# Log-decay rows read back from DRAM instead of picked by matmuls, in a hybrid encoder layer

## The chip, the cores and the metric

The kernel runs on one core of a Trainium2 chip. The metric is the time of one execution on the device in microseconds; the median of several runs is compared. The engines are named as in the profile: PE (TensorE: matmuls; PEld its weight loads), DVE (VectorE), ACT (ScalarE), POOL (GpSimd) and SP (SyncE, which here only issues DMAs). Each engine works through its own instructions in order and waits on semaphores for the others.

## The reference, cut to what matters

One layer of an encoder on 528 tokens (16 learned ones and 512 of input) of width 2048: a normalization, one input projection, three branches (gated linear attention, differential attention, and a Mamba-2 state-space branch, SSD), one output projection and a last normalization. The change lies in the SSD branch: 16 heads in two groups of eight, two directions, chunks of 128 tokens, a depthwise convolution of five taps on 1536 channels.

```python
xbc = silu(depthwise_conv(xbc, conv_w, conv_b))          # 5 taps, 12 tiles of 128 channels
dt = softplus(dt_raw.reshape(B, L, 2, HEADS) + dt_bias)  # one dt per direction and head
a = dt * (-exp(A_log))
y = bidirectional(ssd_chunk_scan, (xs, dt[:, :, 0], a[:, :, 0], Bm, Cm),
                  (xs, dt[:, :, 1], a[:, :, 1], Bm, Cm), SSD_CHUNK)

def ssd_chunk_scan(x, dt, a, Bm, Cm):                    # per chunk of 128
    acs = cumsum(a, axis=2)
    seg = acs[:, :, :, None] - acs[:, :, None, :]
    decay_ts = exp(where(causal, seg, -inf))
    scores = einsum('bctgn,bcsgn->bctsg', Cm, Bm)[..., None] * decay_ts
    y_diag = einsum('bctsgr,bcsgrp->bctgrp', scores, x * dt[..., None])
    ...
```

## The kernel before, in words

The tokens' normalized features are kept transposed, as two float32r parts (`uh` and `ul`, 16 tiles each), so a projection takes three matmuls for each weight tile: high by high, high by low, low by high. Each weight tile is loaded by SP (`wraw`, two buffers), its high part is made on ACT (`whi`, line 72 within `wsplit`) and its low part on DVE (`wlo`, line 146); these two are traced at high priority. `t1` projects 128 columns over all tokens in two chunks of 48 matmuls; `t2` projects 512 columns for 512 tokens.

In the SSD branch the decays of both directions are combined into one tile for each head. `at` is the log decay per token and head. `Xs` holds sums of it with tokens over the partitions, `Xr` the same sums as rows: 32 rows (direction and head) of 512 tokens, as a float32r part and its remainder. In `ssd_decay(g)`, for each of the eight heads of a group:

- POOL makes `dtm`, the tile of dt factors, in two operations of 128 x 512 (lines 439 and 440);
- for each direction a matmul with a one-hot column of `pkr` (line 445) spreads the head's row of `Xr` over all 128 partitions in PSUM;
- for each chunk ACT adds `Xs` of the first direction (line 448), and DVE subtracts that of the second and takes the minimum (line 450);
- ACT takes the exponential (line 452) and DVE multiplies by `dtm` (line 453). The result `m` is kept for the group.

`ssd_group(g, em)` then runs the convolutions, multiplies `m` by the scores (line 552), and computes outputs and states. `conv_tile` copies a projected tile to `xp`, takes the first tap on DVE (line 411), four more taps on DVE (line 413), a tanh on ACT (line 415) and a product on DVE (line 416).

`dtm`, `sg` and most passing tiles of these stages share the tag "w", which has eight slots; `m` has the tag "ya" with twelve. No order is written out by hand: a planner takes the instructions in the program's order as priority, simulates them with its own costs, and fixes each engine's order, SP's queue too. Work that stands later in the program, such as the projections for `z` after the SSD branch, can be put where an engine would be free.

Of the kernel before, what the change touches and what calls it, by code (L numbers as in the profile page):

```python
# [8 lines left out]
F32 = mybir.dt.float32  # L9
F32R = mybir.dt.float32r  # L10
U32 = mybir.dt.uint32
AF = mybir.ActivationFunctionType
ALU = mybir.AluOpType
# [4 lines left out]
P = 128  # L18
NM = 16
S = 512  # L20
L = NM + S
# [6 lines left out]
NC = 4  # L28
# [6 lines left out]
M_ID, M_LE, M_GE, M_ONE, M_DU, M_GT, M_LT, M_LEC, M_GEC = range(9)  # L35


def mm(nc, out, lhsT, rhs, start=True, stop=True):
    nc.tensor.matmul(out, lhsT=lhsT, rhs=rhs, start=start, stop=stop)  # L39
# [2 lines left out]
@with_exitstack  # L42
def encoder_kernel(ctx, tc, x, meta, rel_bias, final_norm_w, norm_w, w_in, w_out, gla_wa2, gla_ba,
                   gla_norm_w, diff_lambda, diff_norm_w, conv_w, conv_b, A_log, dt_bias, ssd_D,
                   ssd_norm_w, masks, umask, onehot, pick, out):
    nc = tc.nc
    ctx.enter_context(nc.allow_low_precision(reason="operands split exactly into two float32r parts"))
    ctx.enter_context(nc.allow_non_contiguous_dma(reason="small parameter rows"))
# [1 line left out]
    const = ctx.enter_context(tc.tile_pool(name="const", bufs=1))  # L50
# [4 lines left out]
    dram = ctx.enter_context(tc.tile_pool(name="dram", bufs=1, space=DRAM))  # L55
# [3 lines left out]
    def pm():  # L59
        return ps_m.tile([P, 512], F32, name="pm", tag="pm")  # L60

    def pb():
        return ps_b.tile([P, 512], F32, name="pb", tag="pb")
# [4 lines left out]
    def slot(tag, shape=None, dt=F32, name=None):  # L68
        return wk.tile(shape or [P, 532], dt, name=name or tag, tag=tag, bufs=BUFS[tag])

    def cpy(out, in_, **kw):
        nc.scalar.activation(out, in_, AF.Copy, **kw)  # L72

    tt = nc.vector.tensor_tensor
    ts_ = nc.vector.tensor_scalar
    stt = nc.vector.scalar_tensor_tensor
    gtt = nc.gpsimd.tensor_tensor
# [33 lines left out]
    mtile = const.tile([P, 5, P], F32, name="masks")  # L111
# [62 lines left out]
    def t1(cols, tokens=True):  # L174

        acc = (pm(), pm()) if tokens else (pm(),)
        for kc in range(2):
            ks = slice(kc * 8, kc * 8 + 8)
            c0 = cols[0][0]
            hi, lo = wsplit(lambda raw: [(raw, win[:, ks, c0:c0 + P])], [P, 8, P])  # L180
            for kk in range(8):
                k = kc * 8 + kk
                for n, (wt, ur) in enumerate(((hi, uh[k]), (hi, ul[k]), (lo, uh[k]))):
                    first = k == 0 and n == 0
                    last = k == KT - 1 and n == 2
                    if tokens:
                        mm(nc, acc[0][:, 0:HA], wt[:, kk, :], ur[:, 0:HA], first, last)
                        mm(nc, acc[1][:, 0:HB], wt[:, kk, :], ur[:, HA:L], first, last)
                    else:
                        mm(nc, acc[0], wt[:, kk, :], ur[:, NM:L], first, last)  # L190
        return acc if tokens else acc[0]

    def take(dst, acc, rows=slice(0, P), **kw):

        cpy(dst[rows, 0:HA], acc[0][rows, 0:HA], **kw)
        cpy(dst[rows, HA:L], acc[1][rows, 0:HB], **kw)
# [112 lines left out]
    nc.sync.dma_start(mtile[:, 1:5], masks[1:5].rearrange("m p q -> p m q"))  # L309
    mstr = slot("w", [P, 4, P], name="mstr")  # L310
    nc.sync.dma_start(mstr, masks[5:9].rearrange("m p q -> p m q"))
    pks = slot("w", [P, 32], name="pks")
    nc.sync.dma_start(pks, pick.rearrange("p z h -> p (z h)"))
    pkr = const.tile([P, 32], F32R, name="pkr")
    cpy(pkr, pks)
    cwx = const.tile([P, 5, 8], F32, name="cwx")
    cwb = const.tile([P, 5, 4], F32, name="cwb")
    cvv = vt[:, 16:76].rearrange("p (k j) -> p k j", j=12)
    cbb = const.tile([P, 12], F32, name="cbb")
# [30 lines left out]
    dtt = const.tile([P, 5, 32], F32, name="dtt")  # L350
# [24 lines left out]
    Xs = const.tile([P, 2, 4, 16], F32, name="Xs")  # L375
    px = pb()
# [1 line left out]
        mm(nc, px[:, z * 64:(z + 1) * 64], mstr[:, 2 + z], at[:, 0:4, z * 16:z * 16 + 16])  # L378
    ts_(Xs[:, 0].rearrange("p c h -> p (c h)"), px[:, 0:64], -1.0, None, ALU.mult)
    nc.vector.tensor_copy(Xs[:, 1].rearrange("p c h -> p (c h)"), px[:, 64:128])  # L380
    Xr = slot("w", [P, S], F32R, name="Xr")
    for z in range(2):
        px = pb()
        for c in range(NC):
            mm(nc, px[0:32, c * P:(c + 1) * P], at[:, c, :], mstr[:, 2 + z])
        zs = slice(32 * z, 32 * z + 32)
        cpy(Xr[zs], px[0:32])
        tt(Xr[64 + 32 * z:96 + 32 * z], px[0:32], Xr[zs].bitcast(F32), ALU.subtract)
    xem = const.tile([NM, 16], F32, name="xem")
    nc.scalar.activation(xem, pd[0:NM, 384:400], AF.Exp)  # L390
    tt(xem, xem, dtt[0:NM, 4, 0:16], ALU.mult)
# [3 lines left out]
    dtd = const.tile([P, 4, 16], F32, name="dtd")  # L395
# [5 lines left out]
    def conv_tile(j, tag, cps=None):  # L401

        if cps is None:
            cps = t1([(C_X + j * P, P, 0)])
        xp = slot("ev", name="xp")
        nc.gpsimd.memset(xp[:, 0:2], 0.0)
        nc.gpsimd.memset(xp[:, 530:532], 0.0)
        take(xp[:, 2:530], cps)
        cw = cwx[:, :, j] if j < 8 else cwb[:, :, j - 8]
        acc = slot(tag, [P, L], name="acc")  # L410
        ts_(acc, xp[:, 0:L], cw[:, 0:1], cbb[:, j:j + 1], ALU.mult, ALU.add)  # L411
        for k in range(1, 5):
            stt(acc, xp[:, k:k + L], cw[:, k:k + 1], acc, ALU.mult, ALU.add)  # L413
        th = slot("ev", [P, L], name="th")
        nc.scalar.activation(th, acc, AF.Tanh, scale=2.0 if j < 8 else 1.0)
        stt(acc, th, 1.0, acc, ALU.add, ALU.mult)
        return acc
# [8 lines left out]
    def bc(ap):  # L426
        return ap[:, :, None].broadcast_to([P, 4, P])
# [5 lines left out]
    def ssd_decay(g):  # L433

        em = []
        for h in range(g * 8, g * 8 + 8):

            dtm = slot("w", [P, 4, P], name="dtm")
            gtt(dtm, mtile[:, None, M_LE, :].broadcast_to([P, 4, P]), bc(dtd[:, :, h]), ALU.mult)
            gtt(dtm, dtm, bc(dtt[:, 0:4, 16 + h]), ALU.add)  # L440

            sg = slot("w", [P, 4, P], name="sg")
            for z in range(2):
                px = pb()
                mm(nc, px, pkr[:, z * 16 + h:z * 16 + h + 1].broadcast_to([P, P]), Xr)
                for c in range(NC):
                    if z == 0:
                        nc.scalar.activation(sg[:, c], px[:, c * P:(c + 1) * P], AF.Identity, bias=Xs[:, 0, c, h:h + 1])
                    else:
                        stt(sg[:, c], px[:, c * P:(c + 1) * P], Xs[:, 1, c, h:h + 1], sg[:, c], ALU.subtract, ALU.min)  # L450
            m = slot("ya", [P, 4, P], name="m")
            nc.scalar.activation(m, sg, AF.Exp)
            tt(m, m, dtm, ALU.mult)  # L453
            em.append(m)
        return em
# [113 lines left out]
    for g in range(2):  # L569
        ssd_group(g, ssd_decay(g))  # L570
# [177 lines left out]
    for g in range(2):  # L748
        snw = slot("st", [P, 512], name="snw")
        nc.gpsimd.dma_start(snw, ssd_norm_w[:, g * 512:(g + 1) * 512].broadcast_to([P, 512]))  # L750
        acc = t2(win, C_Z + g * 512, uh, ul, NM)
# [129 lines left out]
    for o_, i, col in ((og, 0, C_GG), (od, 1, C_DG)):  # L881
        for c in range(NC):
            gtt(v4(o_[c]), v4(o_[c]), gn[:, i][:, None, :].broadcast_to([P, 4, P]), ALU.mult)
        acc = t2(win, col, uh, ul, NM)
# [9 lines left out]
    for k in korder:  # L894
        pt = pb()
        for c in range(NC):
            src, j = (og[c], k) if k < 4 else ((od[c], k - 4) if k < 8 else (yacc[(k - 8) // 4, c], k % 4))
# [29 lines left out]
    for b in range(3):  # L927
        acc = t2(wout, b * 512, mh, ml, 0, korder)
# [6 lines left out]
    acc = [pm() for _ in range(NC)]  # L935
# [40 lines left out]
def _consts():  # L976

    import numpy as np
    i = np.arange(P)
    r, c = i[:, None], i[None, :]  # L980
    masks = np.stack([r == c, r <= c, r >= c, r + c >= 0, r + c >= 0, r > c, r < c,
                      (r <= c) * 1.0 - (r < 64), (r >= c) * 1.0 - (r >= 64)]).astype(np.float32)
    masks[M_DU] = 1.0 + np.eye(P, dtype=np.float32)
    umask = (r > c).astype(np.uint32)
    rel = np.arange(NTAB) - (S + NM - 1)
    n = np.abs(rel)
    nf = np.maximum(n, 1).astype(np.float32)
    large = 8 + (np.log(nf / np.float32(8)) / np.float32(math.log(16.0)) * np.float32(8)).astype(np.int32)
    large = np.minimum(large, 15)
    bucket = np.where(rel > 0, 16, 0) + np.where(n < 8, n, large)  # L990
    onehot = (np.arange(32)[:, None] == bucket[None, :]).astype(np.float32)
    onehot = np.concatenate([onehot, onehot, 0 * onehot])
    pick = np.zeros((P, 2, 16), np.float32)
    for z in range(2):
        for h in range(16):
            pick[48 * z + h, z, h] = pick[64 + 48 * z + h, z, h] = 1.0
    return {'masks': masks, 'umask': umask, 'onehot': onehot, 'pick': pick}


def build(arrays):  # L1000
    import concourse.bacc as bacc
    nc = bacc.Bacc("TRN2", target_bir_lowering=False, num_devices=1, dynamic_dma_scratch_size=8192)
    args = [nc.dram_tensor(k, v.shape, mybir.dt.from_np(v.dtype), kind="ExternalInput").ap()
            for k, v in arrays.items()]
    args.append(nc.dram_tensor("out_0_dram", (S, D), F32, kind="ExternalOutput").ap())
    with tile.TileContext(nc, schedule_with_timeline_sim=True) as tc:
        encoder_kernel(tc, *args)
    return nc
# [10 lines left out]
```

## Time and profile before

| What | Value |
|---|---|
| median of 3 runs | 920.37 us (917.81 to 920.91) |
| profiled execution | 917.57 us, its span 915.8 us |
| PE busy | 876.9 us, 96% |
| DVE busy | 554.0 us, 60% |
| ACT busy | 383.7 us, 42% |
| POOL busy | 183.7 us, 20% |
| moved by DMA | 88.33 MB, mean 96 GB/s |

The span runs from the first to the last instruction of the profiled execution. Busy times are sums over an engine's instructions; matmuls are pipelined, so one record of a matmul is longer than the step from one to the next. The shares are means over stages with different limits.

### The profile page before, as it was taken

What the parts mean: (1) busy time and instruction counts of PE and PEld (TensorE: products, weight loads), DVE (VectorE), ACT (ScalarE), POOL (GpSimd) and SP (SyncE); (2) the same over time, 40 slices, a digit from 0 to 9 for tenths busy, and PEclk for the clock granted to TensorE, in tenths of its full rate; (3) what the DMA queues carried; (4) which work ended last, traced back from release to release, by engine and by line L of the source; (5) the groups of instructions that cost most, each with busy time, mean ns of one, the idle gap of its engine ahead of it and who ended that gap; (6) DMA issues with size and microseconds to landing.
All of it is one profiled execution on the core that took longest, in us unless ns stands there. A gap on an engine that the chain in (4) does not pass through costs nothing.

```text
span 915.8 us, 14461 instructions
## 1 busy us (share of the span) xinstructions
PE 876.9 (96%) x5737; PEld 779.9 (85%) x5737; DVE 554.0 (60%) x1049; ACT 383.7 (42%) x753; POOL 183.7 (20%) x215
## 2 busy tenths in 40 slices
PE   3898999999999999999999999999999999999996
PEld 3898999997778888899999999988888888888884
DVE  6669977999957568853642467775552543232334
ACT  6555434335534376734232345553342333132322
POOL 2006203549246302010040000000120002020200
PEclk9999999999999999999999999999999999999998
DMA  9422332221223234123337333324223532322225
GB/s 238 106 70 69 76 87 71 64 76 46 70 72 91 79 85 115 47 70 93 87 77 203 84 82 84 85 81 136 81 81 103 173 123 90 109 92 92 93 92 184
DMA packets 99587, 88.33 MB, mean 96 GB/s; under 512 B 8223, under 2 KB 75415, under 8 KB 99519
## 3 DMA queue, kind: packets, MB, share of 16 engines
q1 hardware_dynamic: 95183, 77.06, 29.8%
q0 software_dynamic: 1456, 5.10, 1.9%
q10 hardware_dynamic: 2880, 5.24, 1.7%
q8 instruction: 45, 0.74, 0.3%
q14 instruction: 23, 0.19, 0.1%
HBM read 83.18 MB, written 6.34 MB: 98 GB/s over the span
## 4 chain that ended last, share of the span: by engine, by line
PE 75%; DVE 12%; ACT 4%; issue 4%; DMA 2%; SPq 1%; POOL 1%; ACTq 0%; POOLq 0%; DVEq 0%
PE pm L39 65%; PE pb L39 7%; DVE acc L413 2%; DVE wlo L146 2%; DMA xt<-in_x_dram 2%; PE pb L898 1%; PE pb L852 1%; DVE sg L450 1%; ACT whi L72 1%; DVE acc L411 1%; DVE xs L459 1%; DMA gn<-in_diff_norm_w_dram 1%; SPq L228 1%; DVE m L552 1%; DVE m L453 0%
## 5 line engine op out<-in xcount | busy, mean ns | idle before, releaser
L146 DVE TENSOR_TENSOR wlo<-wraw,whi 128x1024 fp32r<-128x1024 f32 (+1 forms) x128 | 163.7, 1280 | 212.6 <-ACT whi L72 212.3
L72 ACT ACTIVATE whi<-wraw 128x1024 fp32r<-128x1024 f32 (+1 forms) x134 | 137.2, 1025 | 297.6 <-PE pm L39 237.4
L39 PE MATMUL pm<-ul,whi 128*128 128x272 f32 (+2 forms) x960 | 224.4, 300 | 0.0
L39 PE MATMUL pm<-uh,whi 128*128 128x272 f32 (+2 forms) x960 | 221.9, 298 | 0.6 <-ACT uh L72 0.6
L39 PE MATMUL pm<-uh,wlo 128*128 128x256 f32 (+2 forms) x928 | 214.6, 297 | 1.2 <-DVE wlo L146 0.7
L39 PEld LDWEIGHTS pm<-uh,whi 128*128 128x128 f32 x960 | 154.8, 189 | 6.7 <-ACT uh L72 1.2
L39 PEld LDWEIGHTS pm<-ul,whi 128*128 128x128 f32 x960 | 155.0, 189 | 5.1 <-issue 0.2
L39 PEld LDWEIGHTS pm<-uh,wlo 128*128 128x128 f32 x928 | 149.7, 189 | 6.8 <-DVE wlo L146 2.1
L39 PE MATMUL pm<-wlo,uh 128*128 128x512 f32 x256 | 102.5, 401 | 2.3 <-DVE wlo L146 2.3
L39 PE MATMUL pm<-whi,ul 128*128 128x512 f32 x256 | 101.3, 397 | 0.0
L39 PE MATMUL pm<-wlo,mh 128*128 128x512 f32 x256 | 100.6, 394 | 0.0
L39 PE MATMUL pm<-whi,ml 128*128 128x512 f32 x256 | 100.5, 394 | 0.0
L39 PE MATMUL pm<-whi,uh 128*128 128x512 f32 x256 | 95.0, 398 | 0.0
L39 PE MATMUL pm<-whi,mh 128*128 128x512 f32 x256 | 90.3, 395 | 0.0
L129 POOL TENSOR_TENSOR rs_r<-rs_v,mhalf 128x1 f32<-128x1 f32 (+1 forms) x28 | 20.5, 734 | 273.2 <-DVE rs_v L128 191.9
L39 PEld LDWEIGHTS pm<-wlo,uh 128*128 128x128 f32 x256 | 48.6, 190 | 13.3 <-DVE wlo L146 2.8
L39 PEld LDWEIGHTS pm<-whi,ml 128*128 128x128 f32 x256 | 48.2, 188 | 11.4
L39 PEld LDWEIGHTS pm<-whi,ul 128*128 128x128 f32 x256 | 48.6, 190 | 10.5
L39 PEld LDWEIGHTS pm<-whi,mh 128*128 128x128 f32 x256 | 48.1, 188 | 11.1
L39 PEld LDWEIGHTS pm<-wlo,mh 128*128 128x128 f32 x256 | 48.1, 188 | 10.9
L39 PEld LDWEIGHTS pm<-whi,uh 128*128 128x128 f32 x256 | 48.2, 189 | 10.7
L932 POOL TENSOR_TENSOR hx<-hx,fw 128x512 f32<-128x512 f32 x12 | 18.1, 1537 | 164.6 <-ACT junk L919 164.6
(304 smaller groups left out, 1197.7 us busy)
## 6 DMA issues: line engine op xcount, KB each, us to landing
wraw<-in_w_in_dram SPq DMA_DIRECT2D x96, 512.0 KB, 3.9
wraw<-in_w_out_dram SPq DMA_DIRECT2D x30, 512.0 KB, 3.6
xt<-in_x_dram SPq DMA_DIRECT2D x16, 256.0 KB, 5.2
hx<-in_x_dram ACTq DMA_DIRECT2D x16, 256.0 KB, 3.9
out_dram<-hx SPq DMA_DIRECT2D x16, 256.0 KB, 2.8
tabr<-tabd POOLq DMA_DIRECT2D x4, 520.0 KB, 7.0
bt<-tabr POOLq DMA_DIRECT2D x4, 456.0 KB, 3.6
fw<-in_final_norm_w_dram ACTq DMA_DIRECT2D x4, 256.0 KB, 4.3
```

Of the source, the lines that this page charges most:

```text
L39: nc.tensor.matmul(out, lhsT=lhsT, rhs=rhs, start=start, stop=stop)
L72: nc.scalar.activation(out, in_, AF.Copy, **kw)
L129: gtt(r[0:rows, 0:cols], v[0:rows, 0:cols], mhalf[0:rows, 0:cols], ALU.pow)
L146: tt(lo, raw, hi.bitcast(F32), ALU.subtract)
L228: nc.sync.dma_start(raw[:, :, 32 * i:32 * i + 32], win[:, k0:k0 + 8, c0:c0 + 32])
L411: ts_(acc, xp[:, 0:L], cw[:, 0:1], cbb[:, j:j + 1], ALU.mult, ALU.add)
L413: stt(acc, xp[:, k:k + L], cw[:, k:k + 1], acc, ALU.mult, ALU.add)
L450: stt(sg[:, c], px[:, c * P:(c + 1) * P], Xs[:, 1, c, h:h + 1], sg[:, c], ALU.subtract, ALU.min)
L459: tt(lo, src, hi.bitcast(F32), ALU.subtract)
L552: tt(m, m, sc, ALU.mult)
L852: nc.tensor.transpose(pt[:, c * P:(c + 1) * P], w_[:, c * P:(c + 1) * P], ident)
L932: gtt(hx[t, b], hx[t, b], fw[b], ALU.mult)
```

## The change

Three edits. The rows of sums are no longer split and kept in SBUF: they are copied to SBUF and written by POOL's DMA queue to a DRAM tile `xd`, 16 rows for each direction. For each head two DMAs on SP's queue read one row each over all 128 partitions, into the tiles `sg` and `sb`; ACT adds to `sg` in place and DVE takes the minimum from both. The one-hot tensor and its tiles are gone. Second, `dtm` is made by four activations on ACT, with a scale and a bias per partition, instead of two operations on POOL. Third, the first tap of each convolution tile is an activation on ACT with scale and bias, instead of an operation on DVE.

```diff
-    pks = slot("w", [P, 32], name="pks")
-    nc.sync.dma_start(pks, pick.rearrange("p z h -> p (z h)"))
-    pkr = const.tile([P, 32], F32R, name="pkr")
-    cpy(pkr, pks)
...
-    Xr = slot("w", [P, S], F32R, name="Xr")
+    xd = dram.tile([32, S], F32, name="xd")
     for z in range(2):
         px = pb()
         for c in range(NC):
             mm(nc, px[0:32, c * P:(c + 1) * P], at[:, c, :], mstr[:, 2 + z])
-        zs = slice(32 * z, 32 * z + 32)
-        cpy(Xr[zs], px[0:32])
-        tt(Xr[64 + 32 * z:96 + 32 * z], px[0:32], Xr[zs].bitcast(F32), ALU.subtract)
+        xf = slot("w", [32, S], name="xf")
+        cpy(xf, px[0:32])
+        nc.gpsimd.dma_start(xd[16 * z:16 * z + 16], xf[16 * z:16 * z + 16])
...
-        ts_(acc, xp[:, 0:L], cw[:, 0:1], cbb[:, j:j + 1], ALU.mult, ALU.add)
+        nc.scalar.activation(acc, xp[:, 0:L], AF.Identity, scale=cw[:, 0:1], bias=cbb[:, j:j + 1])
         for k in range(1, 5):
             stt(acc, xp[:, k:k + L], cw[:, k:k + 1], acc, ALU.mult, ALU.add)
...
             dtm = slot("w", [P, 4, P], name="dtm")
-            gtt(dtm, mtile[:, None, M_LE, :].broadcast_to([P, 4, P]), bc(dtd[:, :, h]), ALU.mult)
-            gtt(dtm, dtm, bc(dtt[:, 0:4, 16 + h]), ALU.add)
-
-            sg = slot("w", [P, 4, P], name="sg")
-            for z in range(2):
-                px = pb()
-                mm(nc, px, pkr[:, z * 16 + h:z * 16 + h + 1].broadcast_to([P, P]), Xr)
-                for c in range(NC):
-                    if z == 0:
-                        nc.scalar.activation(sg[:, c], px[:, c * P:(c + 1) * P], AF.Identity, bias=Xs[:, 0, c, h:h + 1])
-                    else:
-                        stt(sg[:, c], px[:, c * P:(c + 1) * P], Xs[:, 1, c, h:h + 1], sg[:, c], ALU.subtract, ALU.min)
+            for c in range(NC):
+                nc.scalar.activation(dtm[:, c], mtile[:, M_LE, :], AF.Identity, scale=dtd[:, c, h:h + 1],
+                                     bias=dtt[:, c, 16 + h:17 + h])
+
+            sg, sb = [slot("w", [P, 4, P], name=n_) for n_ in ("sg", "sb")]
+            for z, t_ in enumerate((sg, sb)):
+                nc.sync.dma_start(t_.rearrange("p c t -> p (c t)"),
+                                  xd[16 * z + h:16 * z + h + 1, :].broadcast_to([P, S]))
+            for c in range(NC):
+                nc.scalar.activation(sg[:, c], sg[:, c], AF.Identity, bias=Xs[:, 0, c, h:h + 1])
+                stt(sg[:, c], sb[:, c], Xs[:, 1, c, h:h + 1], sg[:, c], ALU.subtract, ALU.min)
             m = slot("ya", [P, 4, P], name="m")
             nc.scalar.activation(m, sg, AF.Exp)
             tt(m, m, dtm, ALU.mult)
```

## Rows read from the trace of the kernel before

**Rows 1.** Busy us (instructions) in stretches: PE, PEld, DVE, ACT, POOL; PEclk, DMA share, GB/s.
```profile
60.00:260.00 200.00, 190.38 (x1549) 177.49 (x1548) 178.57 (x271) 92.61 (x191) 90.80 (x82) 0.99 0.27 72
...
200.00:245.00 45.00, 41.68 (x229) 35.27 (x228) 44.61 (x72) 23.93 (x58) 28.84 (x21) 0.96 0.22 63
```

**Rows 2.** The chain that ended last, in order: start us, us, what.
```profile
217.76 2.07 DVE wlo L146
...
244.07 4.83 DVE m L552 x8
...
740.03 161.32 PE pm L39 x696
```

**Rows 3.** Groups by form, PE: count | busy us, mean ns | idle before, releasers.
```profile
L39 PE MATMUL pb<-Xr,pkr 128*128 128x512 f32 x32 | 11.8, 409 | 3.9 <-DVE Xr L388 2.9 <-DVE sg L450 0.5 <-DVE yo L542 0.5
```

**Rows 4.** Waits of PE, 40 to 260 us: total us, times, longest us.
```profile
PE pm L39 <- DVE wlo L146: 2.3, 1, 2.3
```

**Rows 5.** PE in order of time: start us, us, line, operation.
```profile
230.80 0.50 PE L39 MATMUL pm<-wlo,uh 128*128 128x512 f32 x1 [2.33 <-DVE wlo L146]
...
234.79 0.40 PE L39 MATMUL pm<-whi,ul 128*128 128x512 f32 x1
```

**Rows 6.** ACT in order of time, with the idle time before in brackets.
```profile
76.83 0.64 ACT L415 ACTIVATE th<-acc 128x528 f32<-128x528 f32 x1 [5.65 <-DVE acc L413]
...
83.50 1.14 ACT L448 ACTIVATE sg<-pb,Xs 128x128 f32<-128x128 f32 x4 [0.34 <-PE pb L39]
```

**Rows 7.** Groups by form, DVE, 60 to 260 us.
```profile
L413 DVE SCALAR_TENSOR_TENSOR acc<-xp,cwx,acc 128x528 f32<-128x528 f32 x32 | 29.7, 930 | 0.4
...
L453 DVE TENSOR_TENSOR m<-m,dtm 128x512 f32<-128x512 f32 x16 | 14.8, 924 | 0.3 <-ACT m L452 0.3
...
L411 DVE TENSOR_SCALAR acc<-xp,cwx,cbb 128x528 f32<-128x528 f32 x8 | 7.5, 943 | 0.0
```

**Rows 8.** Single lines and tile m: shortest/median/longest ns, first and last start us.
```profile
L413 DVE SCALAR_TENSOR_TENSOR acc<-xp,cwx,acc x32: 752/767/1799, 90.0 to 232.1; 128x528 f32<-128x528 f32 x32
...
L453 DVE TENSOR_TENSOR m<-m,dtm x16: 676/682/1572, 82.4 to 239.1; 128x512 f32<-128x512 f32 x16
...
L450 DVE SCALAR_TENSOR_TENSOR sg<-pb,Xs,sg x64: 333/339/343, 80.3 to 238.0; 128x128 f32<-128x128 f32 x64
...
L552 DVE TENSOR_TENSOR m<-m,sc x16: 679/686/692, 126.8 to 248.2; 128x512 f32<-128x512 f32 x16
```

**Rows 9.** Groups by form, POOL.
```profile
L440 POOL TENSOR_TENSOR dtm<-dtm,dtt 128x512 f32<-128x512 f32 x16 | 23.6, 1484 | 0.4
L439 POOL TENSOR_TENSOR dtm<-masks,dtd 128x512 f32<-128x512 f32 x16 | 23.2, 1462 | 43.3 <-ACT xp L72 35.5 <-ACT m L452 7.9
```

**Rows 10.** Groups by form, ACT: one operand per partition (two rows), none (last).
```profile
L448 ACT ACTIVATE sg<-pb,Xs 128x128 f32<-128x128 f32 x64 | 18.0, 383 | 0.7 <-PE pb L39 0.7
...
L72 ACT ACTIVATE hx<-hx,r 128x512 f32<-128x512 f32 x8 | 5.3, 716 | 16.5 <-POOL r L962 16.5
...
L641 ACT ACTIVATE E<-E 128x512 f32<-128x512 f32 x4 | 2.5, 629 | 0.0
```

**Rows 11.** DMA issues: count, KB each, median us from issue to landing.
```profile
xt<-in_x_dram SPq DMA_DIRECT2D x16, 256.0 KB, 5.2
...
snw<-in_ssd_norm_w_dram POOLq DMA_DIRECT2D x2, 256.0 KB, 3.7
...
tabd<-tb POOLq DMA_DIRECT2D x2, 8.0 KB, 1.8
```

**Rows 12.** DVE in order of time, 200 to 245 us.
```profile
212.17 2.15 DVE L450 SCALAR_TENSOR_TENSOR sg<-pb,Xs,sg 128x128 f32<-128x128 f32 x8
...
239.11 0.69 DVE L453 TENSOR_TENSOR m<-m,dtm 128x512 f32<-128x512 f32 x1 [0.17 <-ACT m L452]
```

**Rows 13.** SP's issues of line 141: shortest/median/longest ns.
```profile
L141 SPq DMA_DIRECT2D wraw<-in_w_in_dram x94: 367/368/527, 25.5 to 703.0; - x94
```

**Rows 14.** Waits of SP's queue, 20 to 300 us: total us, times, longest us.
```profile
SPq L141 <- DVE wlo L146: 212.6, 31, 11.2
```

More of the change, by code (lines that the diff above doesn't have):

```diff
@@ L44, in encoder_kernel @@
                    gla_norm_w, diff_lambda, diff_norm_w, conv_w, conv_b, A_log, dt_bias, ssd_D,
-                   ssd_norm_w, masks, umask, onehot, pick, out):
+                   ssd_norm_w, masks, umask, onehot, out):
     nc = tc.nc
@@ L992, in _consts @@
     onehot = np.concatenate([onehot, onehot, 0 * onehot])
[L993 to L997, printed above, removed]
+    return {'masks': masks, 'umask': umask, 'onehot': onehot}
 def build(arrays):
```

## The prediction

> **What bounds the kernel now.** I read three views. First the busy time in stretches [rows 1]: between 60 and 260 us, where nearly all the changed lines run, TensorE is busy 190.4 of 200 us, VectorE 178.6, ScalarE 92.6 and GpSimd 90.8. So TensorE has 9.6 us of gaps there, VectorE is nearly full, ScalarE is half empty. In the densest part, 200 to 245 us, VectorE is busy 44.6 of 45 us. Second, the chain of waits in order of time [rows 2]: around 218 to 249 us it runs over VectorE (the low half of a weight tile, line 146; the product of line 552), but its longest piece, 696 matmuls in 161.3 us near the end, is TensorE alone. So VectorE decides locally in the changed stretch, and TensorE over the whole: what leaves TensorE, or its gaps, is time. From the longest piece, one 512-column matmul costs 161.3 / 696 = 0.232 us when nothing waits; the 0.4 us of a single record is pipelined. Third, what TensorE waits for [rows 3 to 5].
>
> **The change part by part.**
>
> *The picking matmuls go.* 32 matmuls of 512 columns [rows 3] at 0.232 us are 7.4 us of TensorE work. They were spread between other matmuls, so this comes off whatever stands behind them. I take **-7.4 us**.
>
> *Waits that can go with them.* In the same row [rows 3] TensorE waits 2.9 us for Xr (line 388) and twice 0.5 us at these matmuls. One wait of 2.3 us is for the low half of a weight tile [rows 4]. After it the records lie wider: from 230.80 to 234.79 us ten matmuls took 3.99 us instead of 2.32 [rows 5], that is the lower of the two clock levels, 1.2 instead of 2.4 GHz, for another 1.7 us; the granted clock of 200 to 245 us is 0.96 [rows 1]. Together 2.9 + 0.5 + 0.5 + 2.3 + 1.7 = 7.9 us. The Xr wait loses its cause; but what stood next there, the weight tile converted on ScalarE, was late too: before the wait ScalarE stood 5.65 us at the tanh of a convolution whose taps VectorE had not finished [rows 6]. Bounds: none of the 7.9 goes, or all. I take half, **-4.0 us**.
>
> *VectorE is relieved.* Eight first taps of x channels took 7.5 us, each 0.94 [rows 7]; with those of the B and C channels about 11 us of VectorE go, and the two subtractions for Xr. Beside that the neighbours speed up. The product of line 453 has a median of 0.68 us, a mean of 0.92 and a maximum of 1.57; line 413 has 0.77, 0.93 and 1.80 [rows 7, 8]. The stretched ones lie where GpSimd runs its two dtm operations per head, 16 x (1.46 + 1.48) = 47 us [rows 9], half of GpSimd's 90.8 [rows 1]. By these two lines alone the excess is 16 x 0.24 + 32 x 0.16 = 9 us; half of it should go. I count no microsecond of this in the sum beyond the half of the waits above: VectorE off the chain gives nothing else.
>
> *ScalarE gets more.* A dtm piece is 128 x 128 with two operands per partition, scale and bias. The row with one such operand is 0.383 us [rows 10]; a scale per partition costs 0.716 - 0.629 = 0.09 at 512 columns [rows 10]. So about 0.44 to 0.47 us, 64 times: 28 to 30 us. A tap of 528 columns by the same rows is 0.63 + 2 x 0.09 = 0.82, 12 times: 10 us. The additions to Xs keep their count; their source moves from PSUM to SBUF, which I cost at nothing (bounds: -0.1 to +0.1 us each, 64 times, on an engine with room). ScalarE goes from 93 to about 131 of 200 us. It is in order, and weight tiles are converted on it, so a burst of dtm pieces can hold a tile back.
>
> The Trainium skill (ScalarE: Activation LUTs, "Rules for kernel authors") says that plain adds and multiplies belong on VectorE, not on ScalarE, so it speaks against this part. Its section "What ACT_TABLE_LOAD costs" prices each per-partition operand at about 93 ns, and the trace agrees (0.716 against 0.629); a dtm piece would then be 0.48 us as an estimate, the 64 pieces 31 us. Followed to its end the rule is the slower rival below.
>
> *The rows by DRAM.* Added are two writes of 16 rows from GpSimd's queue and 32 loads of 256 KB on SP's. The same kind of load (one row of 512 over 128 partitions) landed in 3.7 us, 256 KB tiles under the heavy load of the start in 5.2, a small write to DRAM in 1.8 [rows 11]. For group 0 the first use of the finished tiles is at 126.8 us [rows 8], about 25 us behind the decays, so 1.8 + 3.7 us of latency is covered; without that cover it costs 5.5 us once. For group 1 the last tile comes at 239.1 us and is used at 244.1 [rows 2, 12]: little cover, but the loads can run ahead as far as slots allow. An issue on SP is 0.37 us [rows 13], 32 are 12 us, and SP mostly waits anyway: 212.6 us of 20 to 300 until VectorE had freed a weight buffer [rows 14]. But SP is in order: behind a row load that waits for one of the eight "w" slots (three a head now instead of two, while the lasting slot of Xr is free) stand the loads of weights, then their conversion, then TensorE. A weight chunk is 48 matmuls, some 5.8 us, so a hold of a few us is hidden. Bounds of these new waits, SP's and ScalarE's together: zero, and 15.4 us (the slower rival). I take one wait as long as the longest of TensorE's now, **+2.9 us**, since that row is the nearest.
>
> *The subtraction of line 450* now reads both tensors from SBUF. Its durations were 333 to 343 ns, none stretched [rows 8], while lines 413 and 453, with both inputs in SBUF, stretch.
>
> [...]
>
> By the rows, a stretch doubles an instruction at most; with the 10% that GpSimd stays busy of 200 to 245 us (28.8 less group 1's half of the 47, over 45) [rows 1, 9] it is 64 x 0.34 x 0.1 = 2 us of VectorE, less than the half of the excess that goes.
>
> Sum: -7.4 - 4.0 + 2.9 = **-8.5 us**. The profiled execution took 917.57 us (span 915.8 and 1.77 around it): 909.1. The median of the runs shown, 920.37, stands 2.80 above that execution, so I forecast **912 us** for the median.
>
> **Rivals.**
> *More comes free:* VectorE's relief closes nearly all 9.6 us of gaps: -7.4 - 7.9 = -15.3, 905 us. For it: VectorE's 89% in 60 to 260 us. Against: ScalarE and SP take over duties in the same chain.
>
> *No change:* the row loads give the gain back. If half of the 16 heads hold SP's weight loads past what is hidden, by 1 us each, that is +8 against -7.4: 921 us. For it: three slots a head of eight, and loads that hold a slot for 3.7 us before any work. Against: SP stands idle until buffers are free, and wide gaps lie between weight loads.
>
> *Slower:* ScalarE becomes the bound of the decays. Group 1's first subtraction began at 212.2 us, the last product at 239.1 [rows 12]: 27 us for eight heads. ScalarE would need per head 4 x 0.45 for dtm, 1.14 for the four additions as now [rows 6], and 0.6 for the exponential, 3.5 us, 28 us, with four weight tiles and a tanh 33 us. If TensorE finds its weights late by these 6 us, and then loses 1.7 us of clock, in both groups, that is 2 x 7.7 = 15.4, less 7.4: +8.0, **928 us**. It decides from 7.4 us of new waits on. For it: ScalarE is at 23.9 of 45 us there before the 15 us come [rows 1]. Against: it fits (39 of 45); products of later projections can fill TensorE; dtm pieces need nothing late and can run early.
>
> *Another order:* the program's order is written by the planner from its own costs, so unrelated stages may be arranged anew, by a few us either way; I put it at the slow side of the last rival.
>
> **How the numbers follow.** Forecast 0.50, more comes free 0.12, no change 0.16, slower 0.22. A measurement of this kernel can tell about 0.3%, 2.8 us, from no change. Faster: 0.50 + 0.12 = 0.62; within: 0.16; slower: 0.22. The range reaches from just below "more comes free" (904 us) into the slower rival, to 926 us: outside are its upper half and a little below. The forecast's own range is 906 to 917 us.
>
> **What would show it.** Right: no matmul by pkr, TensorE's work down 7 us, no wait for Xr; line 453 near its 0.68 us throughout; VectorE below 165 us of the 200. Wrong: TensorE waiting longer than 3 us for weight halves between 70 and 260 us; conversions (line 146's source) queued behind dtm pieces; SP's weight loads waiting for slots of sg or sb; the lower clock for more than the 4 us it has now. If TensorE's gaps there grow by over 7 us, the prediction fails.

## The result and the profile after

The changed kernel takes 899.26 us (898.85 to 899.41, 4 runs), the kernel before 920.55 us (917.81 to 920.91): a ratio of 0.9774, 95% interval 0.9755 to 0.9794. That is 21 us in medians, and 18.2 us between the two profiled executions (917.57 and 899.40). The forecast of 912 us had the sign and missed the size; 899 lies below its range.

Of the page of the changed kernel: busy us (share of the span) and count by engine, then the engines' shares of the chain.

```profile
PE 866.4 (97%) x5705; PEld 773.7 (86%) x5705; DVE 536.2 (60%) x1035; ACT 418.8 (47%) x828; POOL 141.1 (16%) x185
...
PE 86%; DVE 5%; ACT 3%; DMA 2%; issue 2%; SPq 1%; ACTq 0%; POOLq 0%; POOL 0%; DVEq 0%
```

The same shares on the page of the kernel before:

```profile
PE 75%; DVE 12%; ACT 4%; issue 4%; DMA 2%; SPq 1%; POOL 1%; ACTq 0%; POOLq 0%; DVEq 0%
```

VectorE's share of the chain fell from 12% to 5%, TensorE's rose from 75% to 86%. TensorE was busy 876.9 us of a span of 915.8 before, 866.4 of 897.6 now: 10.5 us less work and 7.7 us less gap (38.9 to 31.2). Together they are the 18.2 us. The stretches that answer to [rows 1] (same columns):

```profile
60.00:260.00 200.00, 194.56 (x1575) 181.69 (x1575) 162.50 (x264) 131.46 (x274) 50.16 (x53) 1.00 0.41 117
...
200.00:245.00 45.00, 44.05 (x302) 37.16 (x302) 41.94 (x82) 39.04 (x91) 8.80 (x6) 1.00 0.50 150
```

Where TensorE had 9.6 us of gaps it has 5.4, and the granted clock of 200 to 245 us is 1.00 instead of 0.96. VectorE does 16 us less, ScalarE 39 more, GpSimd 41 less. The end of the chain, which answers to [rows 2], is the same piece 17.7 us earlier, so all but 0.5 of the 18.2 us come ahead of it.

```profile
722.30 161.29 PE pm L39 x696
```

TensorE's waits in the whole execution, which answer to [rows 3, 4] (total us, times, longest):

```profile
...
PE pm L39 <- DVE wlo L146: 2.6, 2, 1.7
PE pm L39 <- ACT xp L72: 1.1, 1, 1.1
...
PE pb L39 <- DVE ya L553: 1.0, 1, 1.0
```

The waits for Xr, sg and yo are gone, and between 60 and 260 us none of those left or new exceeds 1.7 us. For weight halves TensorE waits 2.6 us where it waited 3.0 in the whole execution, so most of what went is waits for other things, Xr first. VectorE's groups by form between 60 and 260 us, answering to [rows 7, 8] (line 445 is the subtraction, 448 the product by dtm, 409 the taps):

```profile
L409 DVE SCALAR_TENSOR_TENSOR acc<-xp,cwx,acc 128x528 f32<-128x528 f32 x32 | 26.0, 812 | 5.3 <-ACT acc L407 4.8
L445 DVE SCALAR_TENSOR_TENSOR sg<-sb,Xs,sg 128x128 f32<-128x128 f32 x64 | 18.8, 344 | 7.1 <-DMA sb<-xd 4.4 <-ACT sg L444 1.4 <-ACT m L447 1.3
L448 DVE TENSOR_TENSOR m<-m,dtm 128x512 f32<-128x512 f32 x16 | 11.3, 712 | 0.4 <-ACT m L447 0.3
```

The product went from 0.92 to 0.71 us, the taps from 0.93 to 0.81. What ScalarE took over, answering to [rows 9, 10]:

```profile
L436 ACT ACTIVATE dtm<-masks,dtt,dtd 128x128 f32<-128x128 f32 x64 | 26.7, 484 | 0.0
...
L407 ACT ACTIVATE acc<-xp,cbb,cwx 128x528 f32<-128x528 f32 x8 | 6.6, 824 | 0.3
```

The new loads, answering to [rows 11] (count, KB each, median us to landing), and then SP's waits between 20 and 300 us, answering to [rows 14]:

```profile
sg<-xd SPq DMA_DIRECT2D x16, 256.0 KB, 4.0
sb<-xd SPq DMA_DIRECT2D x16, 256.0 KB, 4.6
```

```profile
SPq L141 <- DVE wlo L146: 153.9, 29, 10.4
...
SPq L441 <- DVE sg L445: 14.7, 9, 5.8
SPq L141 <- DVE sg L445: 12.7, 2, 8.6
...
SPq L441 <- DMA xd<-xf: 7.5, 2, 7.0
```

Row loads (line 441) do wait on SP for slots and for the write of the rows, by up to 7.0 us at a time, and two weight loads (line 141) were held until line 445 was done, by up to 8.6. TensorE's waits above stay short all the same, and SP still idles 154 us for weight buffers.

### The profile page after: what moved, and what is told of

Read it like the earlier page. It is cut to its first block, busy times and chain, and to the rows that moved or that the text cites. A ratio compares the mean times of both kernels' runs of the same rounds, so it can differ in the third digit from the quotient of the medians.

```text
span 897.6 us, 14456 instructions
## 1 busy us (share of the span) xinstructions
PE 866.4 (97%) x5705; PEld 773.7 (86%) x5705; DVE 536.2 (60%) x1035; ACT 418.8 (47%) x828; POOL 141.1 (16%) x185
## 4 chain that ended last, share of the span: by engine, by line
PE 86%; DVE 5%; ACT 3%; DMA 2%; issue 2%; SPq 1%; ACTq 0%; POOLq 0%; POOL 0%; DVEq 0%
PE pm L39 74%; PE pb L39 8%; DMA xt<-in_x_dram 2%; DVE acc L409 1%; DVE wlo L146 1%; PE pb L893 1%; PE pb L847 1%; ACT dtm L436 1%; DMA gn<-in_diff_norm_w_dram 1%; PE pb L279 1%; ACT whi L72 1%; SPq L228 1%; ACT sg L444 0%; DVE sg L445 0%; DVE m L547 0%
## 5 line engine op out<-in xcount | busy, mean ns | idle before, releaser
L39 PEld LDWEIGHTS pm<-whi,ml 128*128 128x128 f32 x256 | 48.2, 188 | 11.3
L39 PEld LDWEIGHTS pm<-wlo,mh 128*128 128x128 f32 x256 | 48.1, 188 | 10.9
```

## The experiments

Differences below are between medians; the kernel before measured 919.7 to 920.7 us in the four jobs, so a few tenths come from there. After the result my theory was that each part has its own price (A); rivals were that the contention of VectorE with GpSimd was the main thing (B), and that the planner's new order was (C).

**The parts, each alone and each taken back.** Each kernel is one of the eight combinations of three edits: R (rows by DRAM), D (dt factors on ScalarE), T (first tap on ScalarE). The edits are the three of the change's diff; the one that matters most below, here alone on the kernel before:

```diff
-            gtt(dtm, mtile[:, None, M_LE, :].broadcast_to([P, 4, P]), bc(dtd[:, :, h]), ALU.mult)
-            gtt(dtm, dtm, bc(dtt[:, 0:4, 16 + h]), ALU.add)
+            for c in range(NC):
+                nc.scalar.activation(dtm[:, c], mtile[:, M_LE, :], AF.Identity, scale=dtd[:, c, h:h + 1],
+                                     bias=dtt[:, c, 16 + h:17 + h])
```

R alone: 

> The kernel before with only the rows by DRAM: the picking matmuls, the one-hot tile and Xr are gone; the dt factors stay on GpSimd and the first tap on VectorE. Whole change: 21 us faster in medians, 18 between the two profiled executions. Theory A (each part its own price): 7.4 us of matmul steps and the 2.9 us wait for Xr go, so 8 to 12 us faster, TensorE's busy time down by 7 to 9 us. Theory B (the contention of VectorE with GpSimd is what mattered): 5 to 8 us faster, since GpSimd's 47 us of dt factors stay and line 450's subtraction now has two inputs in SBUF and is stretched too (mean well above 0.34 us). Theory C (the planner's new order made the gain): anything between 5 us slower and 15 faster, not the sum with the other parts.

D alone: 

> The kernel before with only the dt factors on ScalarE. Theory A: VectorE's stretched neighbours go back (line 453 from 0.92 us to about 0.7), TensorE's gaps between 60 and 260 us shrink by 3 to 5 us of the 9.6: 3 to 7 us faster. Theory B: this is the main part: 10 us faster or more. Theory C: within 5 us either way.

T alone: 

> The kernel before with only the first tap on ScalarE. Theory A: VectorE loses 11 us of work that the chain of waits ran over in part: 1 to 4 us faster. Theory B: no change (within 2 us), the contention stays. Theory C: within 5 us either way.

D and T: 

> The kernel before with the dt factors and the first tap on ScalarE, the picking matmuls kept. Whole change less the rows. Theory A: 5 to 10 us faster, with TensorE's busy time as before and its gaps down by as much; the rows then bring the remaining 10 to 12. Theory B: 13 us faster or more, the rows bring only their 7.4 us of matmuls. Theory C: not near the sum of the two parts alone (off by over 4 us).

R and T: 

> The changed kernel with the dt factors back on GpSimd. Theory A: it loses 3 to 7 us of the change's 21. Theory B: it loses 10 us or more. Theory C: not what dtm_only alone gained (off by over 4 us).

R and D: 

> The changed kernel with the first tap back on VectorE. Theory A: it loses 1 to 4 us of the change's 21. Theory B: within 2 us of the changed kernel. Theory C: not what tap_only alone gained (off by over 4 us).

| Edits | median us | ratio to before, 95% |
|---|---|---|
| R | 915.92 | 0.9953 (0.9934 to 0.9971) |
| D | 908.31 | 0.9870 (0.9847 to 0.9894) |
| T | 914.56 | 0.9940 (0.9924 to 0.9957) |
| D, T | 910.57 | 0.9896 (0.9875 to 0.9916) |
| R, T | 922.39 | 1.0022 (1.0009 to 1.0035) |
| R, D | 905.67 | 0.9838 (0.9821 to 0.9856) |
| R, D, T | 899.26 | 0.9774 (0.9755 to 0.9794) |

D gains on every background: 11.4 us alone, 10.3 beside R, 4.0 beside T, 23.1 beside both. R gains 3.8 alone and 2.6 beside D, loses 7.8 beside T, gains 11.3 beside both. T gains 5.1 alone and 6.4 beside R and D, loses 2.3 beside D and 6.5 beside R. The three parts alone add up to 20.3 us, and the whole is 21.3; D and R together give 14.7 where the two alone make 15.2. The pairs with T don't add: D and T give 9.1 where the two alone make 16.5, R and T lose 2.0 where they make 8.9. So theory A fails on T; B is right on D and wrong on T and on the sum; C's sign, a pair off the sum of its parts by over 4 us, came with these two pairs.

D alone brings most of what the prediction missed. TensorE's gaps are 31.9 us there (span 907.1, busy 875.2), against 38.9 before and 31.2 with the whole change. The wait of 2.9 us for Xr shows how. In both kernels VectorE does the same work in the same order from 59 us up to Xr. First some of it before, and as the last line the weight half that TensorE waited for at 230.80 [rows 4, 5]:

```profile
67.54 1.28 DVE L411 TENSOR_SCALAR acc<-xp,cwb,cbb 128x528 f32<-128x528 f32 x1
68.86 4.38 DVE L413 SCALAR_TENSOR_TENSOR acc<-xp,cwb,acc 128x528 f32<-128x528 f32 x3
...
78.28 0.68 DVE L388 TENSOR_TENSOR Xr<-pb,Xr 32x512 fp32r<-32x512 f32 x1
...
228.68 2.06 DVE L146 TENSOR_TENSOR wlo<-wraw,whi 128x1024 fp32r<-128x1024 f32 x1
```

GpSimd at these times before:

```profile
69.69 2.98 POOL L439 TENSOR_TENSOR dtm<-masks,dtd 128x512 f32<-128x512 f32 x2
72.64 2.52 POOL L440 TENSOR_TENSOR dtm<-dtm,dtt 128x512 f32<-128x512 f32 x2
...
229.74 1.91 POOL L440 TENSOR_TENSOR dtm<-dtm,dtt 128x512 f32<-128x512 f32 x1
```

VectorE with D alone, where GpSimd does nothing from 58.6 to 71.8 us:

```profile
67.40 0.55 DVE L411 TENSOR_SCALAR acc<-xp,cwb,cbb 128x528 f32<-128x528 f32 x1
67.98 2.45 DVE L413 SCALAR_TENSOR_TENSOR acc<-xp,cwb,acc 128x528 f32<-128x528 f32 x3
...
73.88 0.68 DVE L388 TENSOR_TENSOR Xr<-pb,Xr 32x512 fp32r<-32x512 f32 x1
```

The last part of Xr comes 4.4 us earlier, and TensorE's wait for it is gone, though the kernel still has Xr. The wait for the weight half is gone too; before, that half took 2.06 us, and the median of line 146 is 1.23. These are all of TensorE's waits with D alone, 60 to 265 us:

```profile
PE pb L39 <- DVE xs L460: 2.4, 4, 0.9
PE pb L39 <- ACT xs L72: 1.4, 1, 1.4
PE pb L39 <- DVE ya L559: 1.2, 1, 1.2
```

R, which takes away 32 matmuls, is worth little alone. VectorE's groups of that run (60 to 265 us), and TensorE's waits of it:

```profile
L146 DVE TENSOR_TENSOR wlo<-wraw,whi 128x1024 fp32r<-128x1024 f32 x26 | 41.2, 1585 | 8.0 <-ACT whi L72 8.0
L444 DVE SCALAR_TENSOR_TENSOR sg<-sb,Xs,sg 128x128 f32<-128x128 f32 x64 | 32.6, 566 | 3.7 <-DMA sb<-xd 3.7
```

```profile
PE pm L39 <- DVE wlo L146: 12.8, 6, 5.0
```

The subtraction, which now reads two tensors from SBUF, takes 0.566 us in the mean instead of 0.339, 64 times: 14.5 us more of VectorE. The weights' low halves stand in the same queue, and TensorE waits 12.8 us for them. With D the same line takes 0.395 (R and D) and 0.344 (all three). That this stretch is what keeps R's gain small isn't shown: beside D, where it is nearly gone and TensorE waits 2.4 us for weight halves, R gains no more (2.6 us).

**Is it GpSimd's reading?** Both kernels are the changed one with GpSimd loaded again ahead of ScalarE's dt factors, once by the two operations, once by memsets of the same tile:

```diff
             dtm = slot("w", [P, 4, P], name="dtm")
+            gtt(dtm, mtile[:, None, M_LE, :].broadcast_to([P, 4, P]), bc(dtd[:, :, h]), ALU.mult)
+            gtt(dtm, dtm, bc(dtt[:, 0:4, 16 + h]), ALU.add)
             for c in range(NC):
...
+            for _ in range(4):
+                nc.gpsimd.memset(dtm, 0.0)
```

Reading: 

> The changed kernel, where GpSimd again computes each dtm by its two operations, and ScalarE then writes the same tile with the same values: no work is taken from ScalarE, only GpSimd's load comes back. Theory P (VectorE's instructions with two SBUF inputs are held while GpSimd reads SBUF; that interaction is the main thing): line 445's subtraction goes from 0.344 us to 0.5 or more, TensorE waits 10 us or more for weight halves, 12 to 25 us slower than the changed kernel, as with the dt factors on GpSimd alone. Rival O (the order of the planner, or ScalarE's share, makes the difference): under 6 us slower, line 445 below 0.40 us.

Writing: 

> The changed kernel with four memsets of each dtm tile by GpSimd ahead of ScalarE's writes: GpSimd is busy for about as long as with the two operations (4 x 0.5 us a head), in the same place, but reads nothing. Theory P, if it is the reading: line 445 stays below 0.38 us and the kernel within 5 us of the changed one. If any GpSimd work hurts VectorE, or the delay ahead of the dt factors does: as much slower as with the two operations.

Reading: 917.46 us, 18 slower than the changed kernel, ratio to before 0.9968 (0.9955 to 0.9982); TensorE waits 12.6 us for weight halves. Writing: 903.96 us, 4.7 slower, 0.9830 (0.9807 to 0.9852); it waits 3.8. The load isn't quite the same: the two operations kept GpSimd busy 43.6 us, the memsets 32.7. The subtraction's groups, first of the reading kernel, then of the writing one:

```profile
L447 DVE SCALAR_TENSOR_TENSOR sg<-sb,Xs,sg 128x128 f32<-128x128 f32 x64 | 27.3, 479 | 8.0 <-DMA sb<-xd 5.3 <-ACT sg L446 2.7
```

```profile
L447 DVE SCALAR_TENSOR_TENSOR sg<-sb,Xs,sg 128x128 f32<-128x128 f32 x64 | 19.1, 348 | 11.5 <-DMA sb<-xd 5.8 <-ACT sg L446 5.7
```

In order of time it can be seen directly. With R alone, eight subtractions on VectorE, and GpSimd at that time:

```profile
214.48 4.98 DVE L444 SCALAR_TENSOR_TENSOR sg<-sb,Xs,sg 128x128 f32<-128x128 f32 x8
```

```profile
213.35 1.51 POOL L435 TENSOR_TENSOR dtm<-masks,dtd 128x512 f32<-128x512 f32 x1
214.82 1.32 POOL L537 TENSOR_TENSOR ya<-ya,yo 128x512 f32<-128x512 f32 x1
216.11 2.15 POOL L436 TENSOR_TENSOR dtm<-dtm,dtt 128x512 f32<-128x512 f32 x2
```

In the writing kernel, eight subtractions under thirteen memsets:

```profile
205.63 2.18 DVE L447 SCALAR_TENSOR_TENSOR sg<-sb,Xs,sg 128x128 f32<-128x128 f32 x8
```

```profile
205.08 6.37 POOL L436 MEMSET dtm<- 128x512 f32 x13
```

4.98 us against 2.18 for the same eight: VectorE was held while GpSimd ran operations that read, and undisturbed while it only wrote. The mean of 0.479 stays a little under the 0.5 that theory P asked for; its other signs came. The Trainium skill (SBUF — State Buffer, "Who interferes with whom") says just this of VectorE instructions with two SBUF inputs; the trace agrees with it on both sides.

**What GpSimd's dt factors cost, and what they cost ScalarE.** One tile is made ahead of the heads and used by all; the rest is left out:

```diff
+    dtm = const.tile([P, 4, P], F32, name="dtm")
+    for c in range(NC):
+        nc.scalar.activation(dtm[:, c], mtile[:, M_LE, :], AF.Identity, scale=dtd[:, c, 0:1], bias=dtt[:, c, 16:17])
...
-            dtm = slot("w", [P, 4, P], name="dtm")
...
```

From the kernel before: 

> The kernel before with one dtm tile made once (for head 0) and used by all heads, so 15 of the 16 tiles of dt factors are left out, on whatever engine. It prices GpSimd's 47 us without giving ScalarE anything. Theory P: 10 to 16 us faster than before, as with the dt factors on ScalarE (12 us) or a little more, since ScalarE has room. Rival O: 5 us faster or less, or unlike that run by over 5 us.

From the changed kernel: 

> The changed kernel with one dtm tile made once and used by all heads: 60 of ScalarE's 64 activations for dt factors are left out, 25 us of its 27. If ScalarE has become a bound of the decays, as my slower rival said: 4 us faster than the changed kernel or more. If it has room: within 3 us.

907.09 us, 13.1 less than before, 0.9870 (0.9848 to 0.9892): about as much as with D alone (11.4 us less). So D's gain is GpSimd's absence, and ScalarE gives it for 1 to 2 us. Leaving the tiles out also frees a slot a head, which this run doesn't tell apart. From the changed kernel 904.12 us: taking 22 us of work off ScalarE (busy 418.8 to 396.6) gained nothing; it was 4.9 us slower. So ScalarE is no bound of the decays; in the changed kernel's rows above, TensorE's wait for ScalarE is 1.1 us. Why less work is slower wasn't found; TensorE waited 5.8 us for weight halves there, 2.6 in the changed kernel.

**The matmuls by themselves.** 32 matmuls nobody reads, where the picking ones stood:

```diff
+            for z in range(2):
+                px = pb()
+                mm(nc, px, WD, WD[:, None, :].broadcast_to([P, 4, P]))
```

> The changed kernel with 32 matmuls of 512 columns added at the place where the picking matmuls stood, on constants, with no reader and nothing to wait for but a free PSUM buffer. This prices the matmuls alone. If TensorE's work bounds the whole: 7 to 8 us slower than the changed kernel, 0.232 us each. If they were hidden in gaps: under 3 us. If PSUM buffers and the order matter beside the work: over 10 us.

910.14 us, 10.9 slower than the changed kernel, ratio to before 0.9884 (0.9865 to 0.9902). TensorE's work rose by 8.3 us, 0.26 us each (page of this kernel; 866.4 in the changed one):

```profile
PE 874.7 (96%) x5737; PEld 779.7 (86%) x5737; DVE 536.0 (59%) x1035; ACT 418.3 (46%) x829; POOL 141.2 (16%) x185
```

From D and T to the whole change the picking matmuls go, and the work falls from 874.4 to 866.4 us: 8.0. From D to R and D it falls from 875.2 to 868.4: 6.8. Where dt factors stay on GpSimd it falls less, by 4.7 us (R alone) and 3.4 (R beside T), and there the mean granted clock falls as well, to 0.992 and 0.988 from 0.995. So the matmuls' work stands in the time in full. The 10.9 us also pass the 10 that I had set for buffers and order: the gaps grew by 2.5 us beside the work (33.7 against 31.2).

**The read-back's latency.** Every row load issued twice into the same tile:

```diff
                 nc.sync.dma_start(t_.rearrange("p c t -> p (c t)"),
                                   xd[16 * z + h:16 * z + h + 1, :].broadcast_to([P, S]))
+                nc.sync.dma_start(t_.rearrange("p c t -> p (c t)"),
+                                  xd[16 * z + h:16 * z + h + 1, :].broadcast_to([P, S]))
```

> The changed kernel with every row load issued twice into the same tile, the second behind the first's landing on the same queue. This doubles the read-back's latency and holds SP, and the weight loads behind, for some 4 us each. If the read-back is well covered: under 3 us slower than the changed kernel. If SP's order is what my second rival said (weights late behind row loads): 10 to 40 us slower, with TensorE waiting for weight halves between 70 and 110 and between 190 and 235 us.

918.38 us, 19 slower than the changed kernel. TensorE waits 9.7 us for weight halves between 60 and 265 us. SP's waits, 60 to 260 us:

```profile
SPq L443 <- DMA sg<-xd: 32.2, 13, 4.7
SPq L443 <- DMA sb<-xd: 16.5, 13, 5.8
```

So SP's order can do what my "no change" rival said, 49 us of holds; with single loads it doesn't. The second loads also move 8.4 MB more, which this run doesn't tell apart from the holds.

**Order and slots.** Two statements swapped in three kernels (the C channels' convolution traced ahead of the B channels'), and ten slots of tag "w" in the changed one:

```diff
-        BT = conv_tile(8 + g, "st", b_ps if g == 0 else None)
         CT = conv_tile(10 + g, "st")
+        BT = conv_tile(8 + g, "st", b_ps if g == 0 else None)
```

Before: 

> The kernel before with two statements swapped: the C channels' convolution tile is traced ahead of the B channels'. The work is the same, the planner's order is not. It shows how much the order alone is worth. If the order is worth little: within 3 us of the kernel before. If it explains why the parts of the change do not add (they differ from a sum by up to 12 us): 4 to 10 us away from it, in either direction.

Changed: 

> The changed kernel with the same swap. If the order is worth little: within 3 us of the changed kernel. If the changed kernel had a lucky order: 4 to 10 us slower; the change would then be worth less, 11 to 17 us.

R and T: 

> The rows by DRAM and the first tap on ScalarE, dt factors on GpSimd, with the same swap. Without it this kernel was 2 us slower than the kernel before, the worst of the eight combinations. Theory P: the stretch of line 444's subtraction (0.56 us) stays whatever the order, so it stays within 5 us of the kernel before. If its slowness was the order: 8 us faster than the kernel before or more.

Ten slots: 

> The changed kernel with ten slots of tag w instead of eight. TensorE's gaps between 60 and 400 us are 6.3 us; SP's row loads waited some 35 us for slots. If slots still hold the decays back: 2 to 5 us faster than the changed kernel. If not: within 3 us, or the planner's order moves it by up to 5 either way.

The swap moves the kernel before by +0.8 us (921.54; ratio 1.0010, 0.9994 to 1.0026), the changed one by +2.6 (901.86; 0.9806, 0.9780 to 0.9831), R and T by -2.4 (919.96; 0.9994, 0.9977 to 1.0012). So order is worth some 3 us by this swap, not the 20 of the change, and R with T stays slow in another order. Ten slots: 906.43 us, 7 slower than eight, outside all that was expected. Slots don't limit the changed kernel; what the planner then does worse stays open. Theory C falls as the main cause, but the -6.5 to +6.4 us that T is worth are no larger than these 7 us, so T's part may be order alone.

R and T, the slowest of the eight, shows waits for weight halves and the lower clock together. Its stretch (columns as above), then TensorE's waits there:

```profile
60.00:260.00 200.00, 179.04 (x1389) 166.62 (x1390) 176.11 (x247) 100.30 (x198) 86.97 (x81) 0.96 0.38 107
```

```profile
PE pm L39 <- DVE wlo L146: 15.3, 6, 7.0
PE pm L39 <- ACT whi L72: 3.1, 2, 2.7
```

21 us of gaps in 200, and a granted clock of 0.96 besides. Why T makes R worse and R with D better isn't settled: the subtraction is stretched as much with T as without it (0.556 and 0.566 us).

## Why the prediction was wrong, point by point

- **The matmuls, -7.4 us: right.** Their work is 6.8 to 8.3 us by the three pairs of runs with dt factors off GpSimd.
- **The waits, half of 7.9 us, and the new wait of +2.9 us: this failed.** The prediction said "I take half" and priced one new wait as long as TensorE's longest. Measured, gaps fell by 7.7 us, the rest of TensorE's work by some 2.5 (10.5 less 8.0), and between 60 and 260 us no new wait is longer than 1.1. Of the 2.5 us, 1.7 are the stretch at the lower clock behind the wait at 230.80 [rows 5]; the granted clock there is 1.00 now. For the other 0.8 no run shows a cause, and the changed kernel has a stretch at the lower clock of its own (a granted clock of 0.66 from 30 to 35 us). Net -10.2 in place of -1.1. This is nearly all of the 9.7 us between 909.1 and the profiled 899.4.
- **Behind it stands the step on VectorE: "I count no microsecond of this in the sum".** The excess at lines 453 and 413 was read and blamed on GpSimd, and then put at nothing of its own, since "VectorE off the chain gives nothing else". With dt factors off GpSimd and no matmul removed, 11 to 13 us went (D alone, and the single tile), and 7.0 of the 7.7 us of gaps. VectorE makes what TensorE waited for, Xr and a weight half, and GpSimd's work made both late, as the rows at 67 to 78 and at 228 us show. The row was there: 44.6 busy of 45 us [rows 1]. The excess was also read too small: VectorE's work falls by 12.9 us with D alone (554.0 to 541.1), not by half of 9.
- **The subtraction of line 450: right for the whole.** Forecast 2 us in all; 0.3 came (0.344 against 0.339). With GpSimd's dt factors it is 14.5 us, which the prediction didn't say. That "a stretch doubles an instruction at most" was misread: 1.57 against 0.68 and 1.80 against 0.77 [rows 8] are 2.3 times, and with R alone the longest subtraction took 1.36 us, its median 0.34.
- **ScalarE: right.** Forecast 131 of 200 us, and it is 131.5; a tap 0.82 and 0.824; four dtm pieces 1.63 us in a row. The slower rival, ScalarE as the bound of the decays, is refuted: 22 us off ScalarE gained nothing.
- **The rows by DRAM: right.** 4.0 and 4.6 us to landing lie between the bounds 3.7 and 5.2. At single length VectorE waited 4.4 us for them (line 445) and TensorE's waits stayed short; at double length they did not.
- **The rivals.** "More comes free" (905 us) was nearest, with VectorE's 89% for it. It missed 6 us.
- **The signs.** Those named for "right" came: no wait for Xr, the product at a mean of 0.71 us, VectorE at 162.5 of 200. They don't tell -8.5 from -18. Of those for "wrong", weight loads held behind line 445 came (12.7 us), without a long wait of TensorE.
- **The base.** The profiled execution of before was at the low end of its runs, and I added 2.8 us for the median. All runs of the changed kernel lie within 0.6 us of each other; 3.0 us of the 12.7 missed are this. The spread of before goes with the clock: of 23 runs beside the swapped kernels, the three at a mean granted clock of 0.995 took 917.3 to 917.9 us, the six at 0.989 took 920.8 to 923.8. The changed kernel's runs were at 0.995 to 0.998.

## What to carry to other kernels

Where an engine off the main path is full in a stretch and the main engine's inputs pass through its queue, price what its neighbours cost it: instructions with median 0.68 us and mean 0.92 say how much. Before moving a VectorE input from PSUM to SBUF, look at what GpSimd reads at that time. What an edit is worth can hang on the others (the first tap here gave from -6.5 to +6.4 us), so measure them together and apart. A wait of a few us on TensorE costs more than itself where it lowers the clock.

## What the runs showed of the hardware that I had not expected

- VectorE with two SBUF inputs is held by GpSimd's reading and not by its memsets: 0.62 us against 0.27 for the same subtraction in a row of eight.
- A VectorE operation with one SBUF tensor as input can be held too: the first tap (line 411) took 1.28 us at 67.54, with GpSimd at its dt factors, and 0.55 at the same place without them.
- Less work, or more room, isn't always faster under a planner: ScalarE relieved of 22 us gave 904.1 us, two more slots 906.4, against 899.3.
